# A two-layer perceptron on one core: stores of block 0's y all on one queue, mostly ahead of the next block's transposes

## The chip, the cores and the metric

The kernel runs on one core of a Trainium2 chip. The metric is the device time of one execution in microseconds: 851.57 us, the median of 3 runs (851.34 to 853.14).

## What is computed

```python
x: [16, 512, 768], w1: [768, 3072], b1: [3072], w2: [3072, 768], all float32
y = np.maximum(np.matmul(x, w1) + b1, 0)
return np.matmul(y, w2).astype(np.float32)
```

## The kernel before

Both layers run in float16 with float32 sums, as a fast matrix multiplication: a block of operands is cut into parts, sums and differences of the parts are made (`X_SUMS`, `W1_SUMS`, `Y_SUMS`, `W2_SUMS`), 26 products of them are taken where the plain way takes 32, and the products are combined again (`FIRST_OPS`, `SECOND_OPS`). A check of the values' sizes guards this; another path takes over where it fails, which it does not on these inputs.

The 8192 rows of x are 8 blocks of 1024. A block is 8 raw parts in the tile `z`, each of 128 partitions by 768; 19 sums of them (line 815) are made on DVE, and for block 1 those in `X1_POOL` on POOL (GpSimd). w1 is cut into 3 groups of 8 raw parts in the tile `v`, with 18 sums a group (line 829), those in `W1_POOL` on POOL, the others on DVE. For each block and each group, `add_first` issues 26 products of 6 matmuls (line 1142), 256 columns each. ACT and DVE move the results from the 8 banks of `ps` through operations on lines 1165 to 1179, and finished parts of y go to the DRAM tensor `yd` (line 1021). When all 8 blocks are through, the second layer (line 1337) reads y back and stores the output.

Block 0 differs, since at the start the sums of w1 don't exist yet. Its groups 0 and 1 are computed plainly by `plain`: per group 4 strips of w1, per strip 4 products (two halves m of the rows, two halves j of the strip) of 6 or 12 matmuls (line 1040). ACT evicts each product with bias and ReLU (line 1054) into slots 8 to 23 of group 1 of `v`, where w1's sums of that group come later, and two stores per pair of products take it to `yd` (line 1021, in `add_store_y`). There are 32 such stores, 16 a group, and group 1's evictions write the slots that group 0's stores have read. `OUT_ACT` says which stores ACT issues: those of group 1's strips 2 and 3, eight in all; SP issues the other 24. Group 2 of block 0 is already computed by sums, and then block 1 follows with group 0.

Block 1 needs its rows of x the other way round. POOL loads 128 rows at a time (line 728, in `add_load_x`), and SP turns them by a transposing DMA (line 790, in `add_turn`): turns 1 to 8 fill the raw parts in pairs, turns 1 and 2 parts 0 and 1, 3 and 4 parts 2 and 3, 5 and 6 parts 4 and 5, 7 and 8 parts 6 and 7. The sums of block 1 read these parts.

The order on each engine is set by a planner at build time (`Graph`). Every step is a task with an engine, a cost, and what it reads and writes. `run` plays the schedule through with these costs, picks for each engine the most urgent task that can start, and writes the instructions out in that order; on the chip each engine then works through its own list and waits on semaphores. `preset(key, at)` tells the planner that something is there from a given time on; it makes no instruction. A DMA's landing is counted on a semaphore; the transfers of SP and ACT together take eight of these, DMAHW0 to DMAHW7, in turn, in the order in which the planner wrote them, and a transfer waits until the one that took its semaphore before has landed. POOL's transfers have DMASW0 to DMASW7 of their own.

Of the kernel before, what the change touches and what calls it, by code (L numbers as in the profile page):

```python
# [590 lines left out]


EARLY, AHEAD = 4, 8
W1_POOL = ((0, 14), (0, 18), (0, 20), (1, 8), (1, 10), (1, 13), (1, 16), (1, 20), (1, 23), (1, 24), (1, 25), (2, 14))
IN_SLOTS = ()

X1_POOL = (4, 6, 8, 14, 16)
FUSE_V2 = (((0,),), ((1,),), ((2,),))
APART = (0,)
OUT_ACT = lambda g, h, m, r: g == 1 and h > 1  # L600
OUT_POOL = lambda to, u: False

Y_FUSE = ()
# [11 lines left out]
V_QUEUE = "SP"  # L615
EARLY_DUE, EARLY_AT, EARLY_SPARE, T_DMA = 15.0, 0, (4.0, 3.0), 1.0
YS, YL, X_SPARE, YV_SPARE = (460, 0.38), (500, 1.0), 4.0, 1.5
T0_ORDER = (13, 4, 17, 15, 12, 8, 2, 1, 10, 21, 18, 3, 25, 0, 19, 11, 23, 14, 16, 22, 7, 24, 6, 5, 20, 9)
LAST_ORDER = (13, 15, 17, 4, 8, 10, 12, 18, 1, 0, 2, 3, 21, 23, 14, 11, 19, 25, 7, 16, 22, 9, 6,
              24, 20, 5)  # L620
# [3 lines left out]
class Fast:  # L624
# [131 lines left out]
    def presets(self):  # L756
        g = self.g
        at = (9.5, 11.5, 13.5, 15.5, 24.1, 27.1, 30.1, 33.0, 36.0, 39.0, 42.0, 45.0)
        for t in range(12):
            for k in range(2):  # L760
                g.preset(("v", t // 4, 2 * (t % 4) + k), at[t] - (0 if t > 1 or k else 1.0))
        for s in range(4):
            for h in range(2):
                g.preset(("z", NZ - 4 + s, h), 18.6 if s < 2 else 21.2)
            for a in range(2):
                for h in range(2):
                    g.preset(("z", 8 + 2 * s + a, h), (5.3, 5.3, 7.2, 7.2)[s])
        g.preset("b1_rows", 6.0)

# [14 lines left out]
    def add_turn(self, b, s):  # L786
        raw = self.raw_slots(b)
        a = self.rowed[s % len(self.rowed)] if b > 1 else self.rowed1[s]
        self.g.add(
            "SP", 1300, lambda: self.nc.sync.dma_start_transpose(  # L790
                out=self.x_part(b, s), in_=self.z[:, a]), lat=1.6, dma=T_DMA, spare=3 if b > 1 else 1.8,
            reads=self.x_keys(a), writes=[("z", raw[s // 2 * 2 + k], s % 2) for k in range(2)])

    def add_rows(self, b, s):
        self.add_load_x(b, s)
# [7 lines left out]
    def next_x_sums(self, b, limit=99):  # L803

        slot = self.xs[b]
        while self.todo and self.free and limit:
# [4 lines left out]
            a, c, d = slot[o], slot[i], slot[j]  # L811
            e = "POOL" if b == 1 and n in X1_POOL else "DVE"

# [9 lines left out]
    def add_w1_sums(self, g):  # L823
        slot = self.w1s
        for o, i, j, sign in W1_SUMS:
            e = "POOL" if (g, o) in W1_POOL else "DVE"

# [44 lines left out]
    def add_w2_part(self, g):  # L872
# [3 lines left out]
        need = {v for s in left for v in s[1:3]} | set(SECOND_V)  # L876
        first = {SECOND_V[p]: n for n, p in reversed(list(enumerate(T0_ORDER)))}
        for n, s in reversed(list(enumerate(W2_SUMS))):
# [150 lines left out]
    def plain(self, h, j, m, outs, parts=1, split=False, g=0):  # L1029
# [42 lines left out]
        if j:  # L1072
            for r in range(2):
                self.add_store_y(0, 2 * m + r, h, g, reg, r, None if reg else 8 + 8 * m + 4 * r + h,
                                 "ACT" if OUT_ACT(g, h, m, r) else "SP")

# [245 lines left out]
    def add_second(self, t):  # L1322
# [4 lines left out]
        ops = SECOND_OPS  # L1327
        order = T0_ORDER if t == 0 else LAST_ORDER if final else SECOND_ORDER
        slot = self.w2s
# [275 lines left out]
```

## Time and profile before

| | |
|---|---|
| median of 3 runs | 851.57 us |
| the profiled execution | 852.25 us |
| its span, first to last instruction | 850.6 us |
| mean granted TensorE clock | 0.995 |
| busy: PE, DVE, ACT, POOL | 835.0, 702.1, 559.9, 272.3 us |
| share of 16 DMA engines: queue of SP, of POOL, of ACT | 46.2%, 42.9%, 0.7% |

PE is TensorE, DVE VectorE, ACT ScalarE, POOL GpSimd, SP SyncE; PEld is PE's loading of weights. In a timeline, a row has the start and length in us, the engine, the line of the kernel, the operation, output and input, and how many are merged; the bracket has the idle time before it and what ended it. SPq and ACTq are the DMA issues of these engines. Times count from the start of the span. An instruction can show as long while it waits inside.

### The profile page before, as it was taken

How to read it: one execution, taken by the hardware profiler on the slowest of the kernel's cores; microseconds unless marked ns; L12 is line 12 of the kernel's file. 1: busy time of each engine (PE TensorE's matmuls, PEld its weight loads, DVE VectorE, ACT ScalarE, POOL GpSimd, SP SyncE). 2: the span in 40 equal slices, each digit the busy share in tenths (PEclk: the TensorE clock that was granted, in tenths of full speed). 3: DMA queues.
4: the chain of work that ended last, by engine and by line, in shares of the span. 5: the costliest groups of instructions: out<-in, count | busy, mean ns of one | idle time of the engine just before them, and what ended most of it. 6: DMA issues, size and time to landing. Idle time of an engine off the chain costs nothing. (4 is left out here: it accounts for less than half of the span.)

```text
span 850.6 us, 17854 instructions
## 1 busy us (share of the span) xinstructions
PE 835.0 (98%) x6263; PEld 614.1 (72%) x6263; DVE 702.1 (83%) x1320; ACT 559.9 (66%) x1252; POOL 272.3 (32%) x421
## 2 busy tenths in 40 slices
PE   8969999999999999999999999999999999999998
PEld 7628888888888888888876666666656665565664
DVE  5858989798998979889999988788777788777773
ACT  4528878887888778878964555565545468757421
POOL 6445874554655446444413100011000011101000
PEclk9989999999999999999999999999999999999999
DMA  9994999999999989998888989888879899988622
GB/s 218 228 224 109 232 209 237 220 213 241 214 228 215 242 215 244 228 274 275 282 257 203 273 251 284 261 220 230 240 216 275 267 226 229 242 222 272 221 76 76
DMA packets 169168, 193.32 MB, mean 227 GB/s; under 512 B 58556, under 2 KB 144644, under 8 KB 169076
## 3 DMA queue, kind: packets, MB, share of 16 engines
q1 hardware_dynamic: 112480, 119.21, 46.2%
q0 software_dynamic: 54976, 71.00, 42.9%
q10 hardware_dynamic: 1620, 1.95, 0.7%
q8 instruction: 49, 0.80, 0.4%
q14 instruction: 43, 0.35, 0.1%
HBM read 140.39 MB, written 83.95 MB: 264 GB/s over the span
## 5 line engine op out<-in xcount | busy, mean ns | idle before, releaser
L1337 PE MATMUL ps<-v,z 128*128 128x384 f16 x2496 | 407.0, 326 | 0.9 <-ACT ps L1354 0.8
L1142 PE MATMUL ps<-z,v 128*128 128x256 f16 x3432 | 375.0, 273 | 0.0
L1142 PEld LDWEIGHTS <-v 128*128 128x128 f16 x3432 | 335.6, 98 | 39.8 <-issue 0.7
L1337 PEld LDWEIGHTS <-z 128*128 128x128 f16 x2496 | 244.0, 98 | 163.2 <-issue 2.2
L1295 DVE TENSOR_TENSOR z<-z 128x768 f16<-128x768 f16 x448 | 232.9, 553 | 42.9 <-PE ps L1337 27.7
L1021 POOL DMA_DIRECT2D yd<-z x228 | 123.7, 545 | 137.5 <-ACT z L1165 65.1
L1176 DVE CUSTOM_DVE_ANT_0 z<-ps,s 128x512 f16<-128x512 f32 x220 | 145.0, 684 | 25.9 <-PE ps L1142 15.5
L1170 ACT ACTIVATE s<-ps,bt 128x256 f32<-128x256 f32 x352 | 145.1, 473 | 14.9 <-PE ps L1142 8.3
L1354 ACT ACTIVATE s<-ps 128x384 f32<-128x384 f32 (+1 forms) x151 | 73.5, 486 | 122.2 <-PE ps L1337 115.9
L1179 DVE TENSOR_TENSOR s<-ps,s 128x512 f32<-128x512 f32 x132 | 89.5, 684 | 4.9 <-PE ps L1142 4.3
L922 POOL DMA_DIRECT2D z<-in_x_dram x32 | 22.9, 736 | 193.7 <-ACT junk L926 188.5
L815 DVE TENSOR_TENSOR z<-z 128x768 f16<-128x768 f16 x147 | 80.5, 580 | 4.3 <-PE ps L1142 4.1
L926 ACT ACTIVATE junk<-z 128x768 f16<-128x768 f16 x94 | 78.8, 838 | 0.9
L1354 ACT ACTIVATE ps<-ps 128x384 f32<-128x384 f32 x80 | 38.0, 475 | 61.6 <-PE ps L1337 60.9
L1358 DVE TENSOR_TENSOR s<-ps,s 128x384 f32<-128x384 f32 x107 | 59.2, 553 | 13.0 <-PE ps L1337 12.6
L1170 ACT ACTIVATE ps<-ps,bt 128x256 f32<-128x256 f32 x88 | 39.4, 448 | 26.2 <-PE ps L1142 17.0
L1170 ACT ACTIVATE z<-ps,bt 128x256 f16<-128x256 f32 x132 | 54.7, 489 | 2.3 <-PE ps L1142 2.3
L1179 DVE TENSOR_TENSOR ps<-ps,s 128x512 f32<-128x512 f32 x66 | 45.4, 696 | 10.7 <-PE ps L1142 6.2
L1040 PE MATMUL ps<-z,v 128*128 128x256 f16 (+1 forms) x264 | 44.9, 332 | 8.0 <-ACT v L1054 6.4
L1358 DVE TENSOR_TENSOR s<-s,ps 128x384 f32<-128x384 f32 x62 | 34.2, 552 | 21.6 <-PE ps L1337 21.2
L1165 ACT ACTIVATE s<-ps 128x512 f32<-128x512 f32 x66 | 39.8, 602 | 9.8 <-DVE z L1176 6.5
L1165 ACT ACTIVATE z<-ps 128x512 f16<-128x512 f32 x66 | 39.2, 594 | 10.6 <-DVE z L1176 5.0
(59 smaller groups left out, 340.2 us busy)
## 6 DMA issues: line engine op xcount, KB each, us to landing
z<-yd SPq DMA_DIRECT2D x128, 384.0 KB, 6.9
yd<-z POOLq DMA_DIRECT2D x228, 128.0 KB, 3.7
out_dram<-s SPq DMA_DIRECT2D x127, 192.0 KB, 6.2
yd<-z SPq DMA_DIRECT2D x124, 128.0 KB, 3.2
z<-in_x_dram POOLq DMA_DIRECT2D x34, 384.0 KB, 7.7
z<-in_x_dram POOLq DMA_DIRECT2D x56, 192.0 KB, 6.1
v<-w2d SPq DMA_DIRECT2D x36, 192.0 KB, 4.0
w2d<-in_w_dram POOLq DMA_DIRECT2D x24, 192.0 KB, 5.4
```

Of the source, the lines that this page charges most:

```text
L815: (self.nc.gpsimd if e == "POOL" else self.nc.vector).tensor_tensor(out=self.z[:, a], in0=self.z[:, c], in1=self.z[:, d], op=ALU.add if si ...
L926: self.nc.scalar.activation(out=self.junk, in_=src, func=ACTF.Square, accum_out=None if at is None else self.stat[:, at:at + 1])
L1021: {"POOL": self.nc.gpsimd, "SP": self.nc.sync, "ACT": self.nc.scalar}[e].dma_start(out=self.ydram[:, b, slot, g].rearrange("p s m -> p (s ...
L1142: nc.tensor.matmul(pairs(self.ps[:, at, :])[:, :, j], lhsT=self.v[:, g, w, k * self.QM + j * P:k * self.QM + (j + 1) * P], rhs=x.rearrange ...
L1165: nc.scalar.activation(out=out, in_=ps, scale=float(a), func=func if kind == "out" else ACTF.Copy)
L1170: nc.scalar.activation(out=pairs(out)[:, :, j], in_=pairs(ps)[:, :, j], func=func, scale=float(a), bias=self.bt[:, n, g, j:j + 1])
L1176: nc.vector._custom_dve(TENSOR_ADD_SAT, out=out, in0=ps, in1=s, s0=F_MAX, s1=0.0)
L1179: nc.vector.tensor_tensor(out=out, in0=in0, in1=in1, op=ALU.add if a == c else ALU.subtract)
L1295: self.nc.vector.tensor_tensor(out=self.y_view(a), in0=self.y_view(c), in1=self.y_view(d), op=ALU.add if sign > 0 else ALU.subtract)
L1337: nc.tensor.matmul(self.ps[:, bank[ch].at[0], 0:NH], lhsT=self.y_view(ys[SECOND_U[p]])[:, h // 2, h % 2 * P:(h % 2 + 1) * P], rhs=self.v[: ...
L1354: nc.scalar.activation(out=out, in_=ps, func=ACTF.Copy, scale=float(a))
L1358: nc.vector.tensor_tensor(out=out, in0=in0, in1=in1, op=ALU.add if a == c else ALU.subtract)
```

## The change

All of block 0's stores are issued by SP. The planner is told that block 1's turn s (0 to 7) can't start before 47 + s of its own time scale, so it writes the turns behind more of the stores. Two more of w1's sums are POOL's (14 for 12; eight of them are the same), and six of block 1's sums of x for five.

```diff
-W1_POOL = ((0, 14), (0, 18), (0, 20), (1, 8), (1, 10), (1, 13), (1, 16), (1, 20), (1, 23), (1, 24), (1, 25), (2, 14))
+W1_POOL = ((0, 14), (0, 16), (0, 18), (0, 20), (0, 21), (0, 24), (1, 10), (1, 13), (1, 14), (1, 21), (1, 23), (1, 25), (2, 14), (2, 23))
-X1_POOL = (4, 6, 8, 14, 16)
+X1_POOL = (2, 4, 6, 8, 16, 17)
-OUT_ACT = lambda g, h, m, r: g == 1 and h > 1
+OUT_ACT = lambda g, h, m, r: False
+TURN_AT = 47, 1.0
...
+        for s in range(8):
+            g.preset(("turn", s), TURN_AT[0] + TURN_AT[1] * s)
...
-            reads=self.x_keys(a), writes=[("z", raw[s // 2 * 2 + k], s % 2) for k in range(2)])
+            reads=self.x_keys(a) + ([("turn", s)] if b == 1 else []), writes=[("z", raw[s // 2 * 2 + k], s % 2) for k in range(2)])
```

The order of PE's instructions stays the same. After the change line numbers are larger by one to three (1021 becomes 1024, 790 becomes 793, 1054 becomes 1057).

SP's queue around the turns of block 1, before (v holds block 0's plain results, so `yd<-v` is a store of them; z is the tile of x, and `yd<-z` a store of a result by sums):

```order
L1021 DMA yd<-v 128x512 [waits DMAHW3_49,Activation_49]
L1021 DMA yd<-v 128x512 [waits DMAHW4_49]
L790 DMA_TRANSPOSE z<-z 128x6x128 [waits DMAHW5_49,DMASW0_49,PE_49]
L790 DMA_TRANSPOSE z<-z 128x6x128 [waits DMAHW6_49,DMASW1_49]
L790 DMA_TRANSPOSE z<-z 128x6x128 [waits DMAHW7_49,DMASW2_49,PE_49]
L790 DMA_TRANSPOSE z<-z 128x6x128 [waits DMAHW1_49,DMASW3_49]
L790 DMA_TRANSPOSE z<-z 128x6x128 [waits DMAHW3_49,DMASW4_49,PE_49]
L790 DMA_TRANSPOSE z<-z 128x6x128 [waits DMAHW4_49,DMASW6_49,DMASW5_49]
L790 DMA_TRANSPOSE z<-z 128x6x128 [waits DMAHW5_49,DMASW6_49,PE_49]
L790 DMA_TRANSPOSE z<-z 128x6x128 [waits DMAHW7_49,DMASW7_49]
L1021 DMA yd<-z 128x512 [waits DMAHW4_49,DVE_49]
```

The same place after the change, without SP's turns 2 to 7, which stand between the second and the third row:

```order
L1024 DMA yd<-v 128x512 [waits DMAHW6_49]
L793 DMA_TRANSPOSE z<-z 128x6x128 [waits DMAHW7_49,DMASW0_49,PE_49]
...
L793 DMA_TRANSPOSE z<-z 128x6x128 [waits DMAHW6_49,DMASW7_49]
L1024 DMA yd<-v 128x512 [waits DMAHW7_49,Activation_49]
L1024 DMA yd<-v 128x512 [waits DMAHW0_49]
L1024 DMA yd<-v 128x512 [waits DMAHW1_49,Activation_49]
L1024 DMA yd<-z 128x512 [waits DMAHW2_49,DVE_49]
L1024 DMA yd<-v 128x512 [waits DMAHW3_49]
L1024 DMA yd<-v 128x512 [waits DMAHW4_49]
```

Before, 24 stores of v stood ahead of the turns, and two of the eight semaphores between the turns (DMAHW0 and DMAHW2) were taken by stores on ACT. Now 26 stores stand ahead, six behind the turns, and the turns hold all eight semaphores one after another.

ACT at the end of block 0's plain part, before (`v<-ps,b1y` is an eviction):

```order
L1054 ACTIVATE v<-ps,b1y 128x2x2x128 [waits DMAHW2_49,DMAHW1_49,PE_49]
L1054 ACTIVATE v<-ps,b1y 128x2x2x128 [waits PE_49]
L1021 DMA yd<-v 128x512 [waits DMAHW0_49,Activation_49]
L1021 DMA yd<-v 128x512 [waits DMAHW2_49]
L1054 ACTIVATE v<-ps,b1y 128x2x2x128 [waits DMAHW1_49,PE_49]
L1054 ACTIVATE v<-ps,b1y 128x2x2x128 [waits PE_49]
L1021 DMA yd<-v 128x512 [waits DMAHW6_49,Activation_49]
L1021 DMA yd<-v 128x512 [waits DMAHW0_49]
L1054 ACTIVATE v<-ps,b1y 128x2x2x128 [waits DMAHW4_49,DMAHW3_49,PE_49]
```

and after:

```order
L1057 ACTIVATE v<-ps,b1y 128x2x2x128 [waits DMAHW2_49,DMAHW1_49,PE_49]
L1057 ACTIVATE v<-ps,b1y 128x2x2x128 [waits PE_49]
L1057 ACTIVATE v<-ps,b1y 128x2x2x128 [waits DMAHW1_49,DMAHW2_49,PE_49,Activation_49]
L1057 ACTIVATE v<-ps,b1y 128x2x2x128 [waits PE_49,Activation_49]
L1057 ACTIVATE v<-ps,b1y 128x2x2x128 [waits DMAHW4_49,DMAHW3_49,PE_49]
```

The stores between the evictions are gone. What the evictions still wait for is PE and group 0's stores from the same slots, which are among the first sixteen stores of SP's list.

POOL behind the loads of w1's strips, before (`v<-v` is a sum of w1, `z<-in_x_dram` a load of rows, `z<-z` a sum of block 1):

```order
L829 TENSOR_TENSOR v<-v 128x768 x3
L728 DMA z<-in_x_dram 128x768 x7
L829 TENSOR_TENSOR v<-v 128x768
L728 DMA z<-in_x_dram 128x768
L829 TENSOR_TENSOR v<-v 128x768 x4
L1021 DMA yd<-z 128x512 x2
```

and after:

```order
L832 TENSOR_TENSOR v<-v 128x768 x5
L729 DMA z<-in_x_dram 128x768
L832 TENSOR_TENSOR v<-v 128x768
L729 DMA z<-in_x_dram 128x768 x6
L832 TENSOR_TENSOR v<-v 128x768
L729 DMA z<-in_x_dram 128x768
L832 TENSOR_TENSOR v<-v 128x768 x4
L818 TENSOR_TENSOR z<-z 128x768
L1024 DMA yd<-z 128x512 x2
```

Three more sums of w1 stand among the eight loads of rows, two of them ahead of the first, and a sum of block 1 stands ahead of POOL's first stores of y.

## The prediction, made before the changed kernel was run

> **What bounds the kernel now.** The page first: its head, the PE line of the busy times, and the rows of its 40 slices (21.3 us each).
>
> ```profile
> span 850.6 us, 17854 instructions
> PE 835.0 (98%) x6263; PEld 614.1 (72%) x6263; DVE 702.1 (83%) x1320; ACT 559.9 (66%) x1252; POOL 272.3 (32%) x421
> ...
> PE   8969999999999999999999999999999999999998
> ...
> PEclk9989999999999999999999999999999999999999
> ```
>
> TensorE is busy in 98% of the span, so only its idle 15.6 us and stretches at a low clock can be won. One slice stands out, the third (42.5 to 63.8 us): PE 6, granted clock 8. The groups by line say the same: the products of the first layer by sums wait for nothing, those of the second layer 0.9 us in all, and the plain products of block 0 wait 8.0.
>
> ```profile
> L1337 PE MATMUL ps<-v,z 128*128 128x384 f16 x2496 | 407.0, 326 | 0.9 <-ACT ps L1354 0.8
> L1142 PE MATMUL ps<-z,v 128*128 128x256 f16 x3432 | 375.0, 273 | 0.0
> L1040 PE MATMUL ps<-z,v 128*128 128x256 f16 (+1 forms) x264 | 44.9, 332 | 8.0 <-ACT v L1054 6.4
> ```
>
> Then the timeline of PE from 30 to 90 us (start, length, what; idle time before it in brackets):
>
> ```profile
> 29.74 18.29 PE L1040 MATMUL ps<-z,v 128*128 128x512 f16 x84
> 49.57 2.75 PE L1040 MATMUL ps<-z,v 128*128 128x512 f16 x12 [1.54 <-DMA z<-in_x_dram]
> 58.74 5.24 PE L1040 MATMUL ps<-z,v 128*128 128x512 f16 x12 [6.42 <-ACT v L1054]
> 63.81 26.37 PE L1142 MATMUL ps<-z,v 128*128 128x256 f16 x240
> ```
>
> The last strip of block 0's plain part (24 matmuls) is cut in two by waits of 1.54 and 6.42 us, and its second half takes 5.1 us where the first took 2.75. The same time on ACT and on the DMA queues of ACT and SP:
>
> ```profile
> 45.48 0.69 ACT L1054 ACTIVATE v<-ps,b1y 128x512 f16<-128x512 f32 x1 [0.61 <-PE ps L1040]
> 46.20 2.53 ACTq L1021 DMA_DIRECT2D yd<-v  x2
> 46.40 15.08 SPq L790 DMA_TRANSPOSE z<-z  x8
> 48.83 1.26 ACT L1054 ACTIVATE v<-ps,b1y 128x512 f16<-128x512 f32 x2 [2.66 <-DMA yd<-v]
> 56.86 1.02 ACTq L1021 DMA_DIRECT2D yd<-v  x2
> 58.01 1.26 ACT L1054 ACTIVATE v<-ps,b1y 128x512 f16<-128x512 f32 x2 [7.91 <-issue]
> ```
>
> ACT evicts a product every 1.3 us until 45.48. Then it stands 2.66 us over its first two stores of y and 7.91 over the next two. Each time its next eviction (48.83, 58.01) ends its first activation about 0.1 us before PE starts again (49.57, 58.74): PE waits for a bank of ps that ACT has not emptied, the first time too, although that row names a load. Line 790, the turns on SP, names its waiter:
>
> ```profile
> L790 SPq DMA_TRANSPOSE z<-z x8: 1226/1334/4249, 46.4 to 60.2; - x8
> ...
> who waited for it (us, times):
>   ACT v L1054: 7.9, 1
> ...
> DMA to landing us min/median/max: 2.8/3.9/9.7
> ```
>
> So a store on ACT waits for a turn on SP. The orders shown above say why: that store waits on DMAHW6, which the second turn was the last to take, and behind the store stand ACT's evictions, and behind them PE.
>
> The stretches of this wait (columns: length, busy time of PE, PEld, DVE, ACT, POOL, then granted clock, DMA share, GB/s) show the second price:
>
> ```profile
> 52.30:57.00 4.70, 0.02 (x1) 0.00 (x0) 2.38 (x5) 0.00 (x0) 1.12 (x1) 1.00 1.30 198
> 57.00:58.74 1.74, 0.00 (x0) 0.00 (x0) 0.00 (x0) 0.73 (x2) 1.74 (x2) 0.50 1.11 210
> 58.74:63.80 5.06, 5.06 (x12) 1.78 (x12) 0.00 (x0) 1.22 (x2) 0.36 (x1) 0.50 0.97 224
> 63.80:69.00 5.20, 5.20 (x49) 4.64 (x48) 1.55 (x3) 4.95 (x13) 0.58 (x1) 1.00 0.11 38
> ```
>
> The clock falls to 0.50 after 4.7 us of idle PE and is back after 5.06 us of work: twelve matmuls run at half speed.
>
> **The change part by part.**
>
> *ACT's stores go to SP.* With no store left on ACT, its evictions wait for PE and for stores of group 0 that landed long before. PE then runs on: 84 matmuls in 18.29 us are 0.218 each, so the twelve slow ones should take 2.61, not 5.07 (58.74 to 63.81). The gain is 1.54 + 6.42 + (5.07 − 2.61) = 10.4 us. Check: 24 matmuls at 0.218 are 5.2, so block 0's third group starts at 48.03 + 5.2 = 53.2 instead of 63.81, 10.6 earlier; I take 10.4. The four later ACT stores cost PE nothing before (no idle behind 63.81) and give nothing.
>
> Here the Trainium skill speaks against so large a gain. Its first page ("Trainium Kernel Development and Optimization", Key Constraints) says that DMAs from SP, ACT and GpSimd share the same 16 engines and that issuing from several saves the sequencer's issue time alone; by that, the four stores give ACT back 2 × 1.02 us of issue and PE less. The trace has 7.91 us of idle ACT around an issue of 1.02, so here it is the store's own wait that counts, and I keep 10.4.
> On the clock, "TensorE: Matmul & The Clock Gate" (Part 1: The HAM clock gate) gives about 3.4 us of sustained work to return to full rate; by that the slow half would lose about 1.7 us and the sum be 9.7. The rows have 5.06 us at 0.50, and the measurement decides.
>
> *SP takes two more stores ahead of the turns and six behind.* What this queue did before:
>
> ```profile
> 35.89 8.56 SPq L1021 DMA_DIRECT2D yd<-v  x8
> ...
> 58.93 2.56 SPq L790 DMA_TRANSPOSE z<-z  x2
> ...
> yd<-v ACTq DMA_DIRECT2D x2, 128.0 KB, 5.7
> ```
>
> The last two turns were issued by 61.49, so with the shortest landing (2.8) and the median one (3.9) the rows are turned by 63.0 to 64.2. Two more stores ahead cost at least their issue, about 0.4 us each, 0.8 together; at most the turns stand behind their transfer, 5.7 us as the same two took from ACT's queue. Below nothing is possible too, since ACT's packets no longer run beside the turns, but not before the 61.49 of SP's own issue. I take +0.8 (SP's turns did not start to land before the row loads had gone, whatever stood ahead): 63.8 to 65.0. When are they needed? These are DVE's rows, and POOL's first sum of block 1:
>
> ```profile
> 66.09 0.69 DVE L1176 CUSTOM_DVE_ANT_0 z<-ps,s 128x512 f16<-128x512 f32 x1 [11.37 <-PE ps L1142]
> 67.95 0.56 DVE L815 TENSOR_TENSOR z<-z 128x768 f16<-128x768 f16 x1 [1.17 <-PE ps L1142]
> ...
> 75.09 0.55 DVE L815 TENSOR_TENSOR z<-z 128x768 f16<-128x768 f16 x1
> ...
> 73.24 1.64 POOL L815 TENSOR_TENSOR z<-z 128x768 f16<-128x768 f16 x1 [2.46 <-PE ps L1142]
> ```
>
> The sum at 75.09 (9, of raw blocks 5 and 7, from turns 5 to 8) comes 11.3 us behind the group's start, so now at 64.5. The turns land 0.7 before to 0.5 behind that. This is what is late next, once the stall is gone: before, the turns had ten microseconds to spare. A wait of up to 0.5 on DVE would hold PE by less, since eviction has banks in hand; I price it at 0, to 0.5. Sum 10 (67.95 before, 4.1 behind the start) goes to POOL; at 57.3 it may wait a microsecond for turns 3 and 4, and POOL's next sum stands 5 us behind it. The six stores behind the turns are issued by about 64 and free slots of v for group 1's sums, whose products start two groups (2 × 17 us) after 53.2: no cost.
>
> *Three more sums on POOL, three fewer on DVE.* DVE saves 3 × 0.55 of its own time. The price stands in one DVE row, beside POOL's:
>
> ```profile
> 45.74 4.04 DVE L829 TENSOR_TENSOR v<-v 128x768 f16<-128x768 f16 x1
> 46.12 3.24 POOL L829 TENSOR_TENSOR v<-v 128x768 f16<-128x768 f16 x2
> ...
> 39.25 1.74 DVE L829 TENSOR_TENSOR v<-v 128x768 f16<-128x768 f16 x3 [1.27 <-DMA v<-in_w_dram]
> 42.12 12.60 DVE L829 TENSOR_TENSOR v<-v 128x768 f16<-128x768 f16 x15 [1.12 <-DMA v<-in_w_dram]
> ```
>
> A 0.55 us sum lasted 4.04 beside two of POOL: DVE stands still while POOL adds. So three sums move DVE by −1.7 (all hidden) to 3 × 1.62 − 1.7 = +3.2 us. DVE ended its sums at 54.72 and then idled 11.37; its first eviction is now due 2.3 behind 53.2, at 55.5, so the cover shrinks to 0.8 and up to 2.4 could be late, of which the 1.17 idle before 67.95 takes back about half. I take 0, because two of the three run early, where DVE waited 1.27 and 1.12 for strips anyway; the bound is +2.4.
>
> Sum: −10.4. The profiled execution took 852.25 (its span 850.6 and 1.65 around it), so 841.85; the median of the three runs, 851.57, is 0.68 lower: **841.2 us**.
>
> **The rivals.**
>
> *Turns a few us late* (0.14). If they stand behind the two stores for the full 5.7, they land at 68.7 to 69.9, DVE waits 4.2 to 5.4 at its 64.5 sum, evictions stop behind it, and PE loses about as much, at the upper end with the half clock once more (2.5): gain 2.5 to 6.2, time 845.4 to 849. For it: one turn needed 4.25 us to be issued. Against: those late issues fell while row loads held the engines, and these end at the same time.
>
> *DVE late by POOL's sums* (0.07): gain 8.0, 843.6.
>
> *Only issue time is saved* (0.03): ACT loses its stores but its evictions still wait, for stores of group 0. It saves 1.02 us for each of two pairs, of which its usual idle 0.61 before an eviction covered part: 0.8 in all, 850.8. The 7.9 us laid to line 790 speak against it.
>
> *Slower* (0.04): block 1's rows come late at the source. POOL now does three more sums (two ahead of its first row load, one behind it), at 1.65 us or more each about 5 us; the turns wait for those loads in order. With the 5.7 of the stores they land 10.7 later, at 74.9; DVE waits 10.4, PE with it, plus 2.5 for the clock: +2.5 net, 853.7. It turns slower once DVE waits over 7.9 us. Against it, the loads were paced by the strips, not by POOL's work:
>
> ```profile
> 33.54 0.53 POOL L728 DMA_DIRECT2D z<-in_x_dram  x1 [2.89 <-DMA v<-in_w_dram]
> 39.76 0.53 POOL L728 DMA_DIRECT2D z<-in_x_dram  x1 [2.89 <-DMA v<-in_w_dram]
> ```
>
> **How the numbers follow.** The full gain with up to 1 us lost again, 840.5 to 842.2, has 0.72. The range reaches on over the DVE case and a part of the late turns: 840.5 to 844.5. About 0.2% (1.7 us) is what a measurement of this kernel tells from no change. Faster by more: 0.72 + 0.14 + 0.07 = 0.93; within: 0.03; slower: 0.04.
>
> **What would show it.** Right: PE without a gap from 30 us to the end of block 1, third group starting near 53.2, clock 1.00 throughout, no ACT idle over 1 us there, DVE's 11.37 us gone. Wrong: a PE gap behind 53, with DVE waiting for a DMA of z (late turns) or its first eviction later than 55.5 (POOL's sums); or ACT still idle before 53 with no store on it.

## The result, and the profile after

The changed kernel takes 845.23 us (median of 7 executions; six lie between 844.78 and 848.98, and the seventh, 3134.11, is left out of the ratio) beside 851.57 for the kernel before: a ratio of 0.9928, 95% interval 0.991 to 0.9946. It is faster, as forecast, but by 6.3 us instead of 10.4, and the time lies 0.7 above the upper end of the range. The profiled execution took 845.06, with a span of 843.5.

The page first: busy times, PE's and the clock's slices, and the groups of the first layer's two kinds of products.

```profile
PE 833.7 (99%) x6263; PEld 614.7 (73%) x6263; DVE 708.0 (84%) x1317; ACT 560.2 (66%) x1252; POOL 276.4 (33%) x424
...
PE   9999999999999999999999999999999999999997
...
PEclk9999999999999999999999999999999999999999
...
L1145 PE MATMUL ps<-z,v 128*128 128x256 f16 x3432 | 375.8, 273 | 2.6 <-DVE ps L1182 2.5
...
L1043 PE MATMUL ps<-z,v 128*128 128x256 f16 (+1 forms) x264 | 42.1, 321 | 0.0
```

The hole in the third slice is gone, and so is the low clock. The plain products of block 0 (now line 1043) wait for nothing, where they waited 8.0 us. But the products by sums (now line 1145), which waited for nothing before, wait 2.6 us, for DVE's evictions. The timeline of PE says where:

```profile
22.32 30.68 PE L1043 MATMUL ps<-z,v 128*128 128x256 f16 x174
52.84 8.68 PE L1145 MATMUL ps<-z,v 128*128 128x256 f16 x78
62.65 5.40 PE L1145 MATMUL ps<-z,v 128*128 128x256 f16 x48 [1.13 <-DVE ps L1182]
68.56 29.38 PE L1145 MATMUL ps<-z,v 128*128 128x256 f16 x264 [0.51 <-DVE ps L1182]
98.77 11.40 PE L1145 MATMUL ps<-z,v 128*128 128x256 f16 x103 [0.83 <-DVE ps L1182]
```

The third group of block 0 starts at 52.84 instead of 63.81. So 10.97 us were won there, a little more than the forecast's 10.4; the profiled executions differ by 7.19 (852.25 to 845.06). Some 3.8 us were given back: 2.5 in PE's three waits for DVE between 60 and 100 us, and 0.8 because the products by sums took 375.8 us in all for 375.0, which no run explains. The same time on DVE, one row a step:

```profile
55.68 0.68 DVE L1179 CUSTOM_DVE_ANT_0 z<-ps,s 128x512 f16<-128x512 f32 x1
...
59.53 2.46 DVE L832 TENSOR_TENSOR v<-v 128x768 f16<-128x768 f16 x2
61.91 1.28 DVE L1182 TENSOR_TENSOR ps<-ps,s 128x512 f32<-128x512 f32 x2
...
67.34 0.56 DVE L818 TENSOR_TENSOR z<-z 128x768 f16<-128x768 f16 x1 [1.77 <-DMA z<-z]
67.82 0.69 DVE L1182 TENSOR_TENSOR ps<-ps,s 128x512 f32<-128x512 f32 x1
```

The 11.37 us of idle DVE are gone. Two of its sums last 2.46 at 59.53, beside a sum on POOL, and the eviction behind them is the one that PE waits for at 62.65. At 67.34 DVE has waited 1.77 for a turn (z from z by DMA), with PE's next eviction standing behind that sum: PE's 0.51 at 68.56. Before PE's third wait, at 98.77, four sums of DVE beside one on POOL last 4.19; four sums at 75.21 with none beside them last 2.08.

```profile
92.13 4.19 DVE L832 TENSOR_TENSOR v<-v 128x768 f16<-128x768 f16 x4
93.59 1.65 POOL L832 TENSOR_TENSOR v<-v 128x768 f16<-128x768 f16 x1
```

On POOL, the sum that is new there waited for a turn too:

```profile
59.93 1.64 POOL L818 TENSOR_TENSOR z<-z 128x768 f16<-128x768 f16 x1 [1.06 <-DMA z<-z]
```

How full DVE is shows in three stretches, of the kernel before and then of the changed one (columns as in the prediction: busy time of PE, PEld, DVE, ACT, POOL, then clock, DMA share, GB/s):

```profile
42.00:55.00 13.00, 8.78 (x40) 3.81 (x39) 12.46 (x15) 3.66 (x6) 5.98 (x5) 1.00 1.20 229
55.00:66.00 11.00, 7.26 (x32) 3.73 (x32) 0.00 (x0) 3.93 (x8) 3.23 (x2) 0.69 0.85 172
66.00:100.00 34.00, 34.00 (x314) 30.45 (x312) 31.98 (x56) 27.87 (x67) 24.56 (x33) 1.00 0.77 161
```

```profile
42.00:55.00 13.00, 13.00 (x71) 6.84 (x70) 12.73 (x16) 7.52 (x14) 6.22 (x5) 1.00 1.19 224
55.00:66.00 11.00, 9.87 (x91) 8.70 (x90) 9.21 (x14) 8.14 (x21) 8.93 (x9) 1.00 1.11 157
66.00:100.00 34.00, 32.57 (x295) 28.58 (x294) 32.34 (x55) 25.45 (x61) 27.64 (x37) 1.00 0.99 230
```

Before, DVE rested from 54.72 to 66.09, through most of PE's stall and the slow products behind it. After, it is busy 54.28 of 58 us. The DMA engines, too, lose a pause: before, their share was 0.11 from 63.8 to 69.0, and in the last stretch it goes from 0.77 to 0.99.

### The profile page after: what moved, and what is told of

The parts are those of the page before. It is cut to its first block, busy times and chain, and to the rows that moved or that the text cites. A ratio compares the mean times of both kernels' runs of the same rounds, so it can differ in the third digit from the quotient of the medians.

```text
span 843.5 us, 17859 instructions
## 1 busy us (share of the span) xinstructions
PE 833.7 (99%) x6263; PEld 614.7 (73%) x6263; DVE 708.0 (84%) x1317; ACT 560.2 (66%) x1252; POOL 276.4 (33%) x424
## 5 line engine op out<-in xcount | busy, mean ns | idle before, releaser
L1145 PE MATMUL ps<-z,v 128*128 128x256 f16 x3432 | 375.8, 273 | 2.6 <-DVE ps L1182 2.5
L1298 DVE TENSOR_TENSOR z<-z 128x768 f16<-128x768 f16 x448 | 232.7, 552 | 41.0 <-PE ps L1340 29.9
L818 DVE TENSOR_TENSOR z<-z 128x768 f16<-128x768 f16 x146 | 84.6, 612 | 5.3 <-PE ps L1145 2.9
L1043 PE MATMUL ps<-z,v 128*128 128x256 f16 (+1 forms) x264 | 42.1, 321 | 0.0
```

Of the source, the lines that this page charges most:

```text
L818: (self.nc.gpsimd if e == "POOL" else self.nc.vector).tensor_tensor(out=self.z[:, a], in0=self.z[:, c], in1=self.z[:, d], op=ALU.add if si ...
L1145: nc.tensor.matmul(pairs(self.ps[:, at, :])[:, :, j], lhsT=self.v[:, g, w, k * self.QM + j * P:k * self.QM + (j + 1) * P], rhs=x.rearrange ...
L1298: self.nc.vector.tensor_tensor(out=self.y_view(a), in0=self.y_view(c), in1=self.y_view(d), op=ALU.add if sign > 0 else ALU.subtract)
```

## The experiments

Theory S: the old stall was a store in ACT's queue that waited for a turn on a shared DMA semaphore. For what was given back there were two theories: A, turned rows that land late hold DVE and POOL; B, sums on POOL hold DVE still. Each kernel was timed in five rounds beside the kernel before; ratios are to that kernel on the same chip. Rows of PE's timeline are from 20 to 110 us in each.

**Turns alone.** The changed kernel with both sets of sums and this line as before:

```diff
-OUT_ACT = lambda g, h, m, r: False
+OUT_ACT = lambda g, h, m, r: g == 1 and h > 1
```

> The changed kernel with ScalarE's eight stores back on ScalarE and both sets of GpSimd's sums as before: of the change only the later planning of the turns is left. Theory S (the stall was a store in ScalarE's queue that had to wait for a turn with which it shares a DMA semaphore): that store still stands behind the second turn, so ScalarE still idles some 8 us before its eviction, PE about 6.4, and the time is 850.5 to 852.5, as before. Rival (it was the turns' place in time that counted, by the transfers they met): most of the gain is here too, under 847.

It took 852.16 us, ratio 1.0001 (0.9986 to 1.0015). ACT's timeline has the old stall:

```profile
46.38 2.29 ACTq L1024 DMA_DIRECT2D yd<-v  x2
48.78 1.26 ACT L1057 ACTIVATE v<-ps,b1y 128x512 f16<-128x512 f32 x2 [2.43 <-DMA yd<-v]
57.12 1.02 ACTq L1024 DMA_DIRECT2D yd<-v  x2
58.27 1.26 ACT L1057 ACTIVATE v<-ps,b1y 128x512 f16<-128x512 f32 x2 [8.23 <-issue]
```

With the turns planned later but the stores on ACT, nothing is won. On the chip this edit moved the turns little: SP issued them from 46.66 on, before from 46.40. But the rows show what the store waits for. In this kernel, in the one before and in the one with the sums alone, ACT issued the first store of the second pair at 57.12, 56.86 and 56.85, each time 0.07 or 0.08 us after the second turn had landed (57.05, 56.78 and 56.77).

**Stores alone.** The kernel before with this line of the change and no other:

```diff
-OUT_ACT = lambda g, h, m, r: g == 1 and h > 1
+OUT_ACT = lambda g, h, m, r: False
```

> The kernel before with block 0's stores all on SyncE and nothing else: the turns are planned as early as before, so the stores stand between them, and the planner puts sums where it finds room with GpSimd's old sets. Theory S: the stall of PE goes here too, because ScalarE holds no store; the time is at most 846. Theory A (in the changed kernel 1.8 us of the 3.6 given back come from turns that stand behind two more stores and meet GpSimd's transfers): the last turn is issued no later than 61.5 and lands by 65, DVE does not wait for it, and the time is 842.5 to 844. If A is wrong and the sums on GpSimd cost it all (theory B), it is 842 or less. If the stores between the turns hold SyncE, a PE gap stays and it is over 846.

It took 845.24 us, ratio 0.9923 (0.9909 to 0.9936): all of the change's gain, with the turns planned as early as before and the old sums. S holds: the first turns ran where they had run before (issued from 46.02 on), so it was not their place in time that counted. A's number (842.5 to 844) failed, and so did its premise: the stores between the turns delayed them as well, the last was issued at 63.36, and DVE waited 2.4 us for it. PE's rows, from an execution of 849.48, the longest of the five:

```profile
52.68 8.68 PE L1142 MATMUL ps<-z,v 128*128 128x256 f16 x78
63.26 5.40 PE L1142 MATMUL ps<-z,v 128*128 128x256 f16 x48 [1.90 <-DVE ps L1179]
69.77 23.49 PE L1142 MATMUL ps<-z,v 128*128 128x256 f16 x210 [1.12 <-DVE ps L1179]
95.87 14.38 PE L1142 MATMUL ps<-z,v 128*128 128x256 f16 x115 [2.61 <-DVE z L1176]
```

Time is given back near the same places as in the changed kernel, and more of it.

**Old sums.** The changed kernel with `W1_POOL` and `X1_POOL` of before.

> The changed kernel with both sets of GpSimd's sums as before; stores and turns as changed. Theory B (GpSimd's sums, which hold DVE still, gave back 2 us: 1.13 at 62.65 and 0.83 at 98.77): these two PE waits go and the time is 843.0 to 844.0, or less. Theory A (late turns gave it back): they stay or move, since a sum of turned rows goes back to DVE, which now waits for the turns itself: 845 to 847.

845.36 us, ratio 0.9925 (0.9912 to 0.9939), within A's range. B's forecast failed: the wait behind 52.57 became 1.96, not nothing, since DVE now waited for the turn itself.

```profile
52.57 8.68 PE L1145 MATMUL ps<-z,v 128*128 128x256 f16 x78
63.21 15.91 PE L1145 MATMUL ps<-z,v 128*128 128x256 f16 x144 [1.96 <-DVE ps L1182]
80.49 29.68 PE L1145 MATMUL ps<-z,v 128*128 128x256 f16 x269 [1.37 <-DVE z L818]
```

**Sums alone.** The kernel before with `W1_POOL` and `X1_POOL` of the change.

> The kernel before with the changed sets of GpSimd's sums and nothing else: ScalarE's stores and the turns as before. Theory S: the stall stays, and the other sums are hidden behind it: 851 to 852. Theory B: the sums of group 1 behind the stall still cost PE 0.8: 852 to 853. If the sums were the gain: under 849.

854.74 us, ratio 1.0032 (1.0019 to 1.0044), more than either theory gave. The stall stays, and behind it PE waits 1.9 us for DVE (the first of three waits is shown), in spite of DVE's rest from 56.5 to 65.8:

```profile
58.73 4.95 PE L1040 MATMUL ps<-z,v 128*128 128x512 f16 x12 [7.25 <-ACT v L1054]
...
73.31 21.32 PE L1142 MATMUL ps<-z,v 128*128 128x256 f16 x192 [1.11 <-DVE ps L1179]
```

So the new sets cost some 2.7 us with the old stores, and with the new ones nothing that can be measured. They are no gain by themselves.

**No wait for turns.** Neither A nor B had foretold what the sums did, so each suspected cost was taken out of the changed kernel alone, and then both. First the wait:

```diff
-                    out=self.z[:, a], in0=self.z[:, c], in1=self.z[:, d],
+                    out=self.z[:, a], in0=self.v[:, 0, 0] if b == 1 else self.z[:, c], in1=self.v[:, 0, 1] if b == 1 else self.z[:, d],
```

> The changed kernel, but block 1's x sums (on VectorE and on GpSimd) add two strips of weights that have long been there, not turned rows; so block 1's products are of other numbers. Every instruction stays at its place and the turns are made as before; only the sums do not wait for them. Theory A (late turns): VectorE's 1.77 us before its sum at 67.34 and GpSimd's 1.06 before its sum at 59.93 go, PE's wait at 68.56 (0.51, and 0.4 behind it) goes and part of the 1.13 at 62.65: 843.2 to 844.2. Theory B (GpSimd's sums hold VectorE): the 1.13 and the 0.83 at 98.77 stay, and the time is 844.5 or more.

845.35 us, ratio 0.9919 (0.99 to 0.9939). No sum waited for a turn, and the time did not move: A's 843.2 to 844.2 failed, and B's 844.5 or more held. PE's four waits are 0.42, 0.59, 1.31 and 0.87 us, the first three of them:

```profile
61.68 7.37 PE L1145 MATMUL ps<-z,v 128*128 128x256 f16 x66 [0.42 <-DVE ps L1182]
69.63 10.22 PE L1145 MATMUL ps<-z,v 128*128 128x256 f16 x90 [0.59 <-DVE s L1182]
81.16 17.19 PE L1145 MATMUL ps<-z,v 128*128 128x256 f16 x156 [1.31 <-DVE ps L1182]
```

DVE's sums of x, no longer held back, now met POOL's: its 13 between 42 and 100 us took 779 ns each, where they take 548 in the changed kernel. Two of them, beside a sum on POOL at 65.83:

```profile
65.76 2.62 DVE L818 TENSOR_TENSOR z<-v 128x768 f16<-128x768 f16 x2
```

**Small sums on POOL.** The wait for turns stays, but POOL's sums cost DVE next to nothing:

```diff
-                    out=self.z[:, a], in0=self.z[:, c], in1=self.z[:, d],
+                    out=self.z[:, a, 0:w], in0=self.z[:, c, 0:w], in1=self.z[:, d, 0:w],
...
-                    out=self.v[:, g, a], in0=self.v[:, g, b], in1=self.v[:, g, d],
+                    out=self.v[:, g, a, 0:w], in0=self.v[:, g, b, 0:w], in1=self.v[:, g, d, 0:w],
```

with w 8 for POOL's sums of x and of weight groups 1 and 2, those that it made before the change too, and 768 for all others.

> The changed kernel, but GpSimd's x sums and its sums of weight groups 1 and 2 add 8 columns of 768 (the rest of those sums is left out; seven slots are set to zero at the start, while VectorE is idle). The sums keep their places and their waits, and hold VectorE for next to nothing. Theory B: the PE waits at 62.65 (1.13) and 98.77 (0.83) go: 842.8 to 843.5. Theory A: the waits for turns stay, VectorE's 1.77 at 67 among them, and PE's waits at 62.65 and 68.56 with them: 844.3 to 845.0, the 0.83 at 98.77 alone gone.

844.86 us, ratio 0.9921 (0.9893 to 0.9948); single executions from 842.85 to 848.34, so this one is not settled against the changed kernel. The median is in A's range, and of B's forecast the part on the waits came true: those of 62.65 and 98.77 are gone. The groups of DVE between 42 and 100 us, of the changed kernel and then of this one, show what POOL's sums take from DVE's:

```profile
L832 DVE TENSOR_TENSOR v<-v 128x768 f16<-128x768 f16 x25 | 21.1, 893 | 0.7 <-DMA v<-in_w_dram 0.4
```

```profile
L833 DVE TENSOR_TENSOR v<-v 128x768 f16<-128x768 f16 x25 | 12.7, 552 | 1.4 <-DMA v<-in_w_dram 1.2
```

The same 25 sums take 8.4 us less. The Trainium skill ("SBUF — State Buffer", section "SBUF: two separate sides") has these two engines share a pair of ports, which for a DVE instruction with two SBUF inputs is an exclusive lock held for a whole instruction; the rows fit that, 893 ns a sum with POOL's full ones about and 552 without. Most of this was there before the change: 814 ns a sum in the same stretch of the kernel before. DVE used the time to wait for turns (2.4 us) and for stores of y (1.4), and PE's waits moved to 67.30 and 73.79:

```profile
67.30 4.91 PE L1146 MATMUL ps<-z,v 128*128 128x256 f16 x42 [1.08 <-DVE ps L1183]
73.79 36.40 PE L1146 MATMUL ps<-z,v 128*128 128x256 f16 x332 [1.58 <-DVE z L1180]
```

**Both.** No wait for turns, and small sums on POOL.

> Both edits together: block 1's x sums do not wait for turns (they add strips of weights), and GpSimd's sums add 8 columns. If late turns and held sums are all that was given back of the 10.4 us won, PE has no wait of 0.3 us or more between 30 and 110 us, and the time is 841.2 to 842.4, what was forecast with both at nothing. Over 843 there is a third cause.

843.04 us, ratio 0.9901 (0.9878 to 0.9924). PE runs on:

```profile
52.75 18.50 PE L1146 MATMUL ps<-z,v 128*128 128x256 f16 x168
71.43 18.76 PE L1146 MATMUL ps<-z,v 128*128 128x256 f16 x168 [0.18 <-DVE z L1180]
90.44 19.81 PE L1146 MATMUL ps<-z,v 128*128 128x256 f16 x180 [0.25 <-DVE z L1180]
```

No wait reaches 0.3 us. Five of its six executions lie between 842.62 and 843.24, all six of the kernel with only the turns' wait gone between 845.02 and 845.63. Together the two costs are worth 2.3 us beside the latter kernel, and 2.2 beside the changed one's median; the turns' wait alone is worth nothing that can be measured. The median is 0.6 above what was expected and just over the 843 that was to mean a third cause. The two small waits are for evictions that themselves waited for stores of y (2.1 us in four waits on DVE).

**Old x sums.** The changed kernel with `X1_POOL` of before alone.

> The changed kernel with GpSimd's set of x sums as before; its sums of weights, the stores and the turns as changed. The sum of turned rows that stood on GpSimd at 59.93 is VectorE's again. Theory B: without the 1.64 us sum beside VectorE's two the PE wait at 62.65 goes: 843.5 to 844.3. Theory A: VectorE waits for the third and fourth turn itself, as it did with both old sets (1.74 us, PE 1.96): 845 to 846.5.

844.80 us, ratio 0.9914 (0.9892 to 0.9935): between the two forecasts, and not told apart from the changed kernel.

**Short row loads.** Why does the last turn land late? In the changed kernel POOL loads rows of block 2 from 62.62 on; here three of those loads are cut to 64 columns:

```diff
-        m0 = b * self.MB + s * P
+        m0, w = b * self.MB + s * P, 64 if b == 2 and s < 3 else 768
```

> The changed kernel, but block 2's first three row loads on GpSimd (192 KB each, the first issued at 62.62, just behind the last turn's 61.88) carry 64 of 768 columns; so 704 columns of these rows keep old numbers. All instructions keep their places. If the last turn lands late (5.3 us) because it meets these loads: it lands within 4 us, by 66, VectorE's 1.77 us before its sum at 67.34 falls below 0.5, PE's 0.51 at 68.56 goes; the time is 844.3 to 845.2, since VectorE, already behind, makes PE wait somewhere later, as it did where no sum waited for a turn. If the stores of y, not the loads, hold the turn: it lands at 67 as before and nothing moves.

844.10 us, ratio 0.9899 (0.9881 to 0.9918), 0.2 under what was expected. DVE's wait fell to 0.64, not below 0.5: the sum that had started at 67.34 started here at

```profile
64.57 0.91 DVE L818 TENSOR_TENSOR z<-z 128x768 f16<-128x768 f16 x1 [0.64 <-DMA z<-z]
```

and PE ran without a wait to 90 us:

```profile
52.57 37.06 PE L1145 MATMUL ps<-z,v 128*128 128x256 f16 x336
90.77 6.06 PE L1145 MATMUL ps<-z,v 128*128 128x256 f16 x54 [1.14 <-DVE z L1179]
97.85 12.39 PE L1145 MATMUL ps<-z,v 128*128 128x256 f16 x112 [1.02 <-DVE ps L1182]
```

So in this execution the last turn was in by 64.57, 2.8 us earlier than in the changed kernel's profile. That fits the loads being in its way; the next runs show that it is not the whole of it.

**Loads later.** A whole kernel from this: the old x sums, and block 2's row loads planned six products later.

```diff
-X1_POOL = (2, 4, 6, 8, 16, 17)
+X1_POOL = (4, 6, 8, 14, 16)
...
-X1_FROM, X1_LATE, PRE0, PRE0_AT = 4, 2.0, 3, 12
+X1_FROM, X1_LATE, PRE0, PRE0_AT = 4, 2.0, 3, 18
```

> A whole kernel, to be faster: the changed kernel with GpSimd's x sums as before and block 2's first row loads planned six products later, behind the turns. Theory A: the last two turns land by 65.5, VectorE's waits for turns fall from 1.5 to under 0.5, and the time is 843.0 to 844.5, below both kernels. Rival (VectorE has no time left between 42 and 98, so that one wait less shows up as another): 844.5 to 845.5.

843.82 us, ratio 0.9903 (0.9882 to 0.9925). To see whether it beats the changed kernel, both ran once more on one chip.

> The changed kernel once more, unaltered, beside the next one on the same chip: 844.5 to 846, with PE waits of 0.3 to 2 us between 60 and 100 us.

> The changed kernel with GpSimd's x sums as before and block 2's first row loads six products later, once more. If the loads in the turns' way were what could still be won, it is 1 to 2 us under the changed kernel of the same call: 843 to 844.3. If its 843.82 was that chip's, it is within 0.7 of it.

The changed kernel took 845.44 (0.9911, 0.9888 to 0.9934), the one with later loads 843.27 (0.99, 0.9871 to 0.9928). It is 2.2 us ahead there, and its first median was 1.4 below the changed kernel's first; that is about what was expected, but the intervals overlap: probably faster, not proven. DVE still waited 0.5 and 1.0 us for turns in its two profiles, so what it gains is not this wait alone. The changed kernel's second profile (an execution of 846.89) is of use by itself:

```profile
62.52 11.95 PE L1145 MATMUL ps<-z,v 128*128 128x256 f16 x108 [1.08 <-DVE ps L1182]
74.72 5.40 PE L1145 MATMUL ps<-z,v 128*128 128x256 f16 x48 [0.25 <-DVE z L1179]
80.65 11.30 PE L1145 MATMUL ps<-z,v 128*128 128x256 f16 x102 [0.53 <-DVE ps L1182]
93.73 6.05 PE L1145 MATMUL ps<-z,v 128*128 128x256 f16 x54 [1.78 <-DVE z L1179]
100.65 9.55 PE L1145 MATMUL ps<-z,v 128*128 128x256 f16 x86 [0.86 <-DVE ps L1182]
```

Here no DVE sum waited for a turn at all, with the full loads, and yet PE waited 4.5 us. Its 1.08 and 0.86 stand where the first profile has 1.13 and 0.83, after 78 and after 390 products by sums; the other three stand elsewhere, and the 0.51 behind the turn is gone. With later loads PE's waits in this stretch were 0.53 and 0.44.

## Why the prediction was right or wrong

*What bounds the kernel: right.* Only the stall near 50 to 64 us held anything to win. Stores alone won as much as the whole change and turns alone nothing, and the store was issued as the second turn landed: it was ACT's store behind a turn. The rival "only issue time is saved" (850.8) fell. The rule of the Trainium skill ("Trainium Kernel Development and Optimization", Key Constraints) by which issuing from several engines saves issue time alone does not speak of a store that waits in its queue; here that wait counted, 7.91 us beside 1.02 of issue.

*The sum's large term, 10.4: right.* The third group starts at 52.84, forecast 53.2; 10.97 us were won up to there. The clock is at full rate throughout, so the 2.46 us for the slow half belonged in the sum.

*Turns +0.8 us late, priced at 0 (to 0.5): too small in one profile of two.* The last two were to land between 63.8 and 65.0; DVE's sum got its rows at 67.34 in the changed kernel's first profile, but by 64.7 in its second one. In the first the eight issues ended at 63.15, 1.7 us later than before (61.48) instead of 0.8; in the second at 62.16, 0.7 later, as forecast:

```profile
46.91 16.24 SPq L793 DMA_TRANSPOSE z<-z  x8
```

What was not reckoned with is that the group that starts 11 us earlier brings its own transfers (POOL's stores of y, block 2's loads) beside the turns. Before, these came when the turns were done: the DMA share had fallen to 0.11 from 63.8 to 69.0. That they hold the last turn is argued from this; the run with short loads fits, but the second profile has full loads too, so it stays open how much they do.

*POOL's three more sums, priced at 0 (bound 2.4): not refuted, but the wrong question.* The check that was made held: DVE's first eviction came at 55.68, due at 55.5. With the new stores the old sets are no faster (845.36), so moving three sums cost nothing that can be measured. But the cover was looked for only up to that eviction. All of POOL's sums, those of before too, run until 98 us, and DVE's slowed sums in there have evictions behind them. PE's waits after 78 and 390 products by sums stand in both profiles of the changed kernel and without the waits for turns, and are gone in both kernels with small sums; with short loads, the first of them is missing too.

*"Eviction has banks in hand": the step that failed.* The late turn was priced at 0 with these words, since a wait of DVE was to reach PE only in part, and POOL's sums because DVE was covered up to its first eviction. Both took DVE to have time in hand behind the stall. It had next to none: it was busy 54.28 of 58 us, and PE waited for its evictions 2.5 us in the first profile and 4.5 in the second. The two things that the sum had at nothing, the wait for turns and the holding by POOL's sums (those of before included), together cost about 2.2 us: without both it is 843.04, and PE's two waits are 0.43 in all. What each costs is only half known. Without the waits for turns alone it stays at 845.35. Without the holding by POOL alone the median is 844.86, but three of its six executions lie between 842.85 and 844.26 and three between 845.47 and 848.34, so it is not shown that the two costs do not add.

The loss does not hang on the other two parts of the change: the kernel with the stores alone has neither the moved sums nor the later planning of turns, and it ends at 845.24 too. So it came with the end of the stall, which had hidden what DVE lacked. That DVE's rest in the stall was the reserve is argued from this, and it is not the whole: with the sums alone DVE rested there too, and PE waited 1.9 us for it all the same.

*The rivals.* "Turns a few us late" (845.4 to 849) came near in its number, and its wait is there (1.77 and 1.06 us), as is the sign of being wrong that the forecast named, a gap of PE behind 53 with DVE waiting for a DMA of z; but by itself that wait is not the cause. "DVE late by POOL's sums" (843.6) named the other cost. Neither stood for both together. (In "Slower", 851.57 + 2.5 is 854.1, not 853.7; nothing hangs on it.) With both costs out, 843.04 is still 1.8 above 841.2. The kernel before had 852.11 in that call, 0.5 more than 851.57; PE's two waits are 0.43 in all, and its products by sums took 375.6 us for 375.0. The rest stays open. No run took away DVE's waits for stores of y (2.1 us).

## What to carry over

When a stall is removed, ask what each engine did in it. An engine that rested there may have no such rest afterwards, and the stage behind must be read anew: its busy share without the pause, and the transfers that now fall together. Where one engine is at 94% of a stage, do not price its delays at nothing because one cover is found; and to learn what two of them cost, take out each, and both together, before judging either.

## What the runs showed that was not expected

- A transfer in one queue can wait for a transfer in another whose semaphore it takes: with these stores on ACT, its eviction stood some 8 us behind one of them, with the turns planned early or late alike (7.91, 8.23 and 8.73 us in three kernels).
- POOL's sums make DVE's sums of weights 60% longer over a whole stage (893 ns for 552), although POOL adds for only 23.4 of its 58 us.
- Executions of one kernel differ in where PE waits. The changed kernel's two profiles (845.06 and 846.89) share two places, after 78 and after 390 products by sums; one wait of the first and three of the second stand alone. The long execution of the kernel with the stores alone (849.48 where the median is 845.24) has 2.61 us of PE's wait at 95.87, with 3.5 us of DVE's waits for stores of y to land. Why such stores land late in one execution and not in another was not tried.
